# Block products in a feed-forward layer: sums of weight blocks on GpSimd, three pairs of k tiles instead of two

## Chip, cores and metric

One core of a Trainium2 chip runs the whole program: a two-layer encoder in float32, batch 1, 256 tokens, model width 2048. The metric is the device time of one execution in microseconds (us), the median of the runs shown.

## What is computed

The reference, cut to what the change touches. Before these lines each layer has three token mixers side by side (chunkwise mLSTM, latent attention, dilated attention) that share one input projection `w_in` and one output projection `w_out`.

```python
def hybrid_layer(x, ...):
    h = rms_norm(x, norm_mix)
    z = jnp.einsum('bsd,de->bse', h, w_in)
    ...                                   # the three mixers give y
    x = x + jnp.einsum('bse,ed->bsd', y, w_out)
    h = rms_norm(x, norm_ff)
    u = jax.nn.relu(jnp.einsum('bsd,df->bsf', h, w_ff1))
    return x + jnp.einsum('bsf,fd->bsd', u * u, w_ff2)
```

`w_ff1` is 2048 x 8192 and `w_ff2` 8192 x 2048, in each of two layers.

## The kernel before

**Products.** Every float32 operand is split into a high part that TensorE (PE) takes at full rate (`F32R`) and a remainder; a product is the three matmuls high x high, high x remainder, remainder x high. For the weights, `Weights.split` does this: ScalarE (ACT) casts a loaded unit `wst` (128 x 1024) to `whi`, VectorE (DVE) subtracts to get `wlo`. There are three buffers `wst` (`B_ST`) and four of `whi` and `wlo` each (`B_HL`), so the split of a unit can start once PE has used the unit four places before it. SyncE's queue (SP) issues the loads in the order of `weight_order`.

**Feed-forward.** `ffn` runs over four chunks of 2048 hidden columns. In a chunk, FF1 makes 16 tiles of 128 hidden columns, f0 to f15, each from two half units of `w_ff1` (`w_half`); `ff1_end` squares the ReLU, scales it and splits it into `u`. FF2 then makes four column groups of 512 output columns. The chunk is "quick" (`fast`) in three chunks of layer 0 and four of layer 1, and there two column groups are made at a time by `fast_groups`: g (left) and g+1 (right), each with two banks of PSUM, one for each half of the tokens.

**Block products.** For a pair `kp` of k tiles the product of a 2 x 2 block matrix of activations (two token halves by two k tiles) and a 2 x 2 block matrix of weights (two k tiles by two column groups) takes eight block products. For the pairs in `FAST = (2, 5)` it is made with seven, of sums of blocks: `act_sums` makes four sums of activation blocks on DVE, and `split` makes four sums of weight blocks, t1 to t4, on DVE from the blocks `a` (unit of the left group, "first") and `b` (unit of the right group, "second"). These make two more units to split, "sums" (t1, t2) and "more sums" (t3, t4). Four of the seven products gather in four banks `fast`, over both pairs, and at the end `fast_end` adds them to `x`, eight additions on DVE and one copy on ACT. The other six pairs are made plainly by `token_group`.

**Order.** The instructions of each engine stand in the order in which the program issues them. A planner (`Stream`) sets it at build time: it holds tasks with due times, worked out from a table of costs, and after each matmul it issues the tasks that are due. In `fast_groups` before, the left group runs through all pairs in order with both block pairs in their places, and then the right group runs through its six plain pairs.

Of the kernel before, what the change touches and what calls it, by code (L numbers as in the profile page):

```python
# [69 lines left out]
MARGIN = 0.3  # L70
ML_AT_ONCE = 2
WARM = 10
# [149 lines left out]
class Weights:  # L222
# [3 lines left out]
    def __init__(self, c, items):  # L226
        self.c, self.items = c, items
        self.srcs = [(i, src, n) for i, (src, n, kind) in enumerate(items) if src is not None]
        self.st, self.hl = {}, {}
        self.i = self.d = self.k = 0  # L230

    def load(self):
        c = self.c
        if self.d == len(self.srcs):
            return
        i, src, n = self.srcs[self.d]
        self.st[i] = c.wp.tile([P, 1024], F32, tag="wst", name="wst", bufs=c.B_ST)
        for cols in self.pieces(i):
            c.nc.sync.dma_start(self.st[i][:, cols], src[:, cols])
        self.d += 1  # L240

# [5 lines left out]
    def split(self):  # L247

        c, nc, k = self.c, self.c.nc, self.k
        src, n, kind = self.items[k]  # L250
        hi = c.wp.tile([P, 1024], F32R, tag="whi", name="whi", bufs=c.B_HL)
        lo = c.wp.tile([P, 1024], F32R, tag="wlo", name="wlo", bufs=c.B_HL)
        if kind == "sums":
            a, b = self.st.pop(k - 2), self.st.pop(k - 1)

            x, y = (c.big.tile([P, 1040], F32, tag="big", name="ws") for _ in range(2))
            self.st[k + 1] = y
            pieces, st = [slice(0, 512), slice(512, 1024)], x
        else:
            st = self.st[k] if kind else self.st.pop(k)  # L260
            if kind == "second":
                st = st[:, 512:]
                pieces = [slice(0, 512)]
            elif kind == "more sums":
                st = self.st.pop(k)
                pieces = [slice(0, 512), slice(512, 1024)]
            else:
                pieces = self.pieces(k)

        def parts():  # L270
            if kind == "sums":
# [5 lines left out]
            for cols in pieces:  # L277
                nc.scalar.copy(hi[:, cols], st[:, cols])
            yield
            for cols in pieces:  # L280
                nc.vector.tensor_tensor(out=lo[:, cols], in0=st[:, cols], in1=hi[:, cols].bitcast(F32),
                                        op=ALU.subtract)

        t = c.s.spawn(parts())
        if kind != "more sums":
            c.s.step(t)
        else:
            t.due = max(t.due, self.sums.due)
        if kind == "sums":
            self.sums = t  # L290
        self.hl[k] = (hi, lo, t)
        self.k += 1

    def next(self):
        while self.k < min(len(self.items), self.i + self.c.B_HL - 1):
            loads = self.items[self.k][0] is not None
            self.split()
            if loads:
                self.load()
        hi, lo, t = self.hl.pop(self.i)  # L300
        self.c.s.finish(t)
        self.i += 1
        return hi, lo
# [3 lines left out]
FAST = (2, 5)  # L307


def fast(l, ch, depth):  # L310
    return l == depth - 1 or ch < NCHUNK - 1


def weight_order(c, depth):
    srcs = []
    for l in range(depth):
# [8 lines left out]
        for ch in range(NCHUNK):  # L325
# [4 lines left out]
            for g in range(0, NX, 2):  # L330
                for kp in range(KT // 2):
                    if kp in FAST:
                        srcs += [(c.w_ff2[l, ch, g, kp], 1024, "first"), (c.w_ff2[l, ch, g + 1, kp], 1024, "second"),
                                 (None, 1024, "sums"), (None, 1024, "more sums")]
                    else:
                        srcs.append((c.w_ff2[l, ch, g, kp], 1024))
                srcs += [(c.w_ff2[l, ch, g + 1, kp], 1024) for kp in range(KT // 2) if kp not in FAST]
# [235 lines left out]
def layer_tables(c):  # L573
# [3 lines left out]
    rope = c.cp.tile([P, 4, NT, MLA_ROPE], F32, tag="rope", name="rope", bufs=1)  # L577
    drope = c.cp.tile([P, 2, NT, 4, DIL_ROT], F32, tag="drope", name="drope", bufs=1)
# [85 lines left out]
def k_rope(c, z1):  # L664
# [18 lines left out]
    kh = c.cp.tile([P, S], F32R, tag="krh", name="krh", bufs=1)  # L683
    kl = c.cp.tile([P, S], F32R, tag="krl", name="krl", bufs=1)
# [206 lines left out]
def ml_gates(c, z1):  # L891
# [60 lines left out]
    ahl = c.cp.tile([P, 2, S], F32R, tag="ml_ahl", name="ml_ahl", bufs=1)  # L952
# [171 lines left out]
def mixers(c, prepare, after):  # L1124
    nc, s = c.nc, c.s
    dv = c.cp.tile([P, 2, NT, DIL_H * DIL_DH], F32R, tag="dv", name="dv", bufs=1)
# [96 lines left out]
def ffn(c, l, last_layer, depth):  # L1223
# [3 lines left out]
    c.xss = new_ss(c)  # L1227
    for ch in range(NCHUNK):
# [3 lines left out]
        sums = {}  # L1232
        for f in range(KT):
# [5 lines left out]
            if i and kp in uf:  # L1239
                c.s.spawn(act_sums(c, us, kp, uf[kp], sums))  # L1240
        for g in range(0, NX, 2):
            last = last_layer and ch == NCHUNK - 1 and g == NX - 2
            if quick:
                fast_groups(c, us, sums, l, ch, g, last, last_layer, nxt)
# [8 lines left out]
def act_sums(c, us, kp, u, sums):  # L1253
# [5 lines left out]
    sf = tile2k(c, "sf", F32)  # L1259
# [5 lines left out]
    hl = c.big.tile([P, 1040], F32R, tag="big", name="s_hl")  # L1265
# [6 lines left out]
def fast_groups(c, us, sums, l, ch, g, last, last_layer, nxt):  # L1272
# [12 lines left out]
    banks = None  # L1285
    for kp in range(KT // 2):
        if kp not in FAST:
            token_group(c, us, left, 512, [kp])
            continue
        first, end = kp == FAST[0], kp == FAST[-1]  # L1290
        if first:
            right = two_banks(c)
            c.s.until(lambda: c.s.room["m"] >= 4)
            c.s.give(m=-4)
            banks = [new_bank(c, "fast") for _ in range(4)]
        p1, q5, p6, p7 = banks
        c.s.until(lambda: kp in sums)
        s1, s2, s3, s4 = sums[kp]
        w = c.w.next()
        product(p1, u(2 * kp, 0), w, one, first, end)  # L1300
        product(left[0], u(2 * kp + 1, 0), w, two, False, False)
        w = c.w.next()
        product(right[0], s4, w, one, first, False)
        w = c.w.next()
        product(q5, s1, w, one, first, end)
        product(p6, s2, w, two, first, end)
        w = c.w.next()
        product(p7, s3, w, one, first, end)
        product(left[1], u(2 * kp + 1, 1), w, two, False, False)
        if end:  # L1310
            done = c.s.spawn(fast_end(c, banks, g))
    c.s.spawn(ff2_end(c, left, g, l, ch, last_layer, nxt, done))
    kps = [kp for kp in range(KT // 2) if kp not in FAST]
    token_group(c, us, right, 512, kps[:-1] if last else kps, opened=(0,))
    if last:
        last_unit(c, us, right, 512)
    c.s.spawn(ff2_end(c, right, g + 1, l, ch, last_layer, nxt, done))

# [69 lines left out]
def encoder(ctx, tc, xT, x, const, vecs, w_in, w_in1, w_mla, w_out, w_ff1, w_ff2, out):  # L1388
# [31 lines left out]
    c.mean = c.cp.tile([P, 16], F32, tag="mean", name="mean")[:, :2]  # L1420
# [165 lines left out]
```

## Time and profile before

| | us |
|---|---|
| median of three runs (2107.16 to 2109.35) | 2108.2 |
| the profiled execution | 2108.59 |
| its span | 2106.8 |
| PE busy in it | 2094.5 |
| DVE busy | 1582.6 |
| ACT busy | 1125.8 |
| GpSimd (POOL) busy | 13.8 |
| DMA | 389.91 MB, mean 185 GB/s |

The profile is one execution; the quick chunks repeat each other, so that rows of one stand for all. Busy time is the time in which an engine had at least one instruction running; matmuls overlap, so that the duration of one (0.39 us for 512 columns) is longer than its distance from the next.

### The profile page before, as it was taken

The numbers are of one execution on the slowest core, as the hardware profiler recorded it, in microseconds if no ns is written. First come the engines' busy times: TensorE is split into PE (matmuls) and PEld (weight loads), VectorE is DVE, ScalarE is ACT, GpSimd is POOL, SyncE is SP. The second block draws the span as 40 slices with busy tenths as digits, with TensorE's granted clock in tenths as the row PEclk, the third lists the DMA queues.
The fourth block names the chain that finished last, engine by engine and source line by source line (L and its number), as shares of the span: only waits on it lengthen the run. The fifth ranks groups of instructions, "written<-read, shape, count | busy, mean of one in ns | idle before, by whom it ended". The sixth has DMA issues, their size and how long they took to land.

```text
span 2106.8 us, 29301 instructions
## 1 busy us (share of the span) xinstructions
PE 2094.5 (99%) x10792; PEld 1791.9 (85%) x10792; DVE 1582.6 (75%) x2624; ACT 1125.8 (53%) x1870; POOL 13.8 (1%) x35
## 2 busy tenths in 40 slices
PE   9999999999999999999999999999999999999999
PEld 8888888888888888888888888888888888888887
DVE  6789865788778778775557888567877787787786
ACT  5777654454455444544456675554544454454453
POOL 1000000000000000001000000000000000000000
PEclk9999999999999999999999999999999999999999
DMA  7544455666656665656555445556665566666665
GB/s 264 162 169 156 150 170 181 194 189 204 191 182 200 200 191 183 210 192 200 181 170 166 140 137 165 175 180 193 190 203 191 178 206 199 189 191 201 190 193 176
DMA packets 109151, 389.91 MB, mean 185 GB/s; under 512 B 12368, under 2 KB 12496, under 8 KB 108752
## 3 DMA queue, kind: packets, MB, share of 16 engines
q1 hardware_dynamic: 107136, 384.71, 57.8%
q10 hardware_dynamic: 1872, 3.33, 0.4%
q8 instruction: 84, 1.38, 0.3%
q14 instruction: 59, 0.48, 0.1%
HBM read 385.90 MB, written 2.10 MB: 184 GB/s over the span
## 4 chain that ended last, share of the span: by engine, by line
PE 95%; DMA 2%; DVE 1%; ACT 1%; issue 0%; ACTq 0%; DVEq 0%
PE g L200 85%; PE fast L200 4%; PE mla_z L200 2%; DMA wst<-w_in 1%; PE oT L200 1%; DVE wlo L104 1%; PE mla_s L200 1%; ACT whi L104 1%; PE ml_h L200 1%; PE pT L206 0%; PE xT L206 0%; PE dil_s L200 0%; DMA wst<-w_ff 0%; PE nkT L206 0%; PE dqkT L206 0%
## 5 line engine op out<-in xcount | busy, mean ns | idle before, releaser
L104 ACT CAST whi<-wst 128x1024 fp32r<-128x1024 f32 (+3 forms) x733 | 749.0, 1025 | 394.5 <-PE g L200 181.8
L104 DVE TENSOR_TENSOR wlo<-wst,whi 128x1024 fp32r<-128x1024 f32 (+3 forms) x733 | 863.6, 1189 | 127.4 <-ACT whi L104 125.5
L200 PE MATMUL g<-whi,u 128*128 128x512 f32 x1712 | 539.9, 390 | 0.0
L200 PE MATMUL g<-xg,whi 128*128 128x512 f32 x2048 | 489.9, 391 | 0.0
L200 PEld LDWEIGHTS g<-xg,whi 128*128 128x128 f32 x2048 | 376.7, 188 | 72.6
L200 PEld LDWEIGHTS g<-whi,u 128*128 128x128 f32 x1712 | 321.6, 188 | 66.7
L200 PE MATMUL g<-whi,xg 128*128 128x512 f32 (+1 forms) x1152 | 371.7, 389 | 1.8 <-ACT whi L104 1.8
L200 PE MATMUL g<-wlo,u 128*128 128x512 f32 x856 | 333.4, 389 | 0.0
L200 PEld LDWEIGHTS g<-xg,wlo 128*128 128x128 f32 x2048 | 262.9, 191 | 11.7 <-ACT xg L104 2.0
L200 PE MATMUL g<-xg,wlo 128*128 128x256 f32 x2048 | 267.4, 283 | 1.1 <-ACT xg L104 1.1
L200 PEld LDWEIGHTS g<-whi,xg 128*128 128x128 f32 x1152 | 215.2, 189 | 39.2 <-ACT whi L104 2.0
L200 PE MATMUL g<-wlo,xg 128*128 128x512 f32 (+1 forms) x576 | 221.0, 384 | 2.4 <-DVE wlo L104 2.4
L104 ACT COPY junk<-g 128x256 f32<-128x256 f32 x128 | 47.8, 373 | 304.9 <-PE g L200 304.9
L200 PEld LDWEIGHTS g<-wlo,u 128*128 128x128 f32 x856 | 160.9, 188 | 33.4
L104 DVE TENSOR_TENSOR junk<-g,junk 128x256 f32<-128x256 f32 x128 | 54.3, 424 | 173.8 <-ACT junk L104 173.8
L200 PE MATMUL g<-whi,y 128*128 128x512 f32 x512 | 164.7, 394 | 0.0
L200 PEld LDWEIGHTS g<-wlo,xg 128*128 128x128 f32 x576 | 109.2, 190 | 20.1 <-DVE wlo L104 3.8
L200 PEld LDWEIGHTS g<-whi,y 128*128 128x128 f32 x512 | 96.2, 188 | 19.4
L200 PE MATMUL g<-wlo,y 128*128 128x512 f32 x256 | 99.8, 390 | 0.0
L104 DVE TENSOR_TENSOR x<-g,x 128x512 f32<-128x512 f32 x80 | 53.4, 688 | 55.6 <-PE g L200 55.6
L104 ACT CAST whi<-ws 128x512 fp32r<-128x512 f32 x112 | 63.8, 619 | 40.5 <-PE g L200 40.5
L104 DVE TENSOR_TENSOR wlo<-ws,whi 128x512 fp32r<-128x512 f32 x112 | 71.7, 687 | 3.7 <-ACT whi L104 1.5
(244 smaller groups left out, 1693.1 us busy)
## 6 DMA issues: line engine op xcount, KB each, us to landing
wst<-w_ff SPq DMA_DIRECT2D x512, 512.0 KB, 4.2
wst<-w_in SPq DMA_DIRECT2D x127, 512.0 KB, 3.6
wst<-w_out SPq DMA_DIRECT2D x64, 512.0 KB, 4.0
wst<-w_in SPq DMA_DIRECT2D x16, 336.0 KB, 3.1
wst<-w_mla SPq DMA_DIRECT2D x12, 416.0 KB, 3.2
x<-x SPq DMA_DIRECT2D x2, 1024.0 KB, 6.0
out<-x ACTq DMA_DIRECT2D x8, 256.0 KB, 2.5
xt<-xT SPq DMA_DIRECT2D x7, 256.0 KB, 6.7
```

The costliest lines, as they stand in the source:

```text
L104: return fn(*args, **kw)
L200: c.nc.tensor.matmul(out, lhsT, rhs, start=start, stop=stop)
```

## The change

The third pair: `FAST` is (1, 3, 5). `fast_groups` no longer runs the left group to its end first, but follows the table `FAST_ORDER`: l is a plain unit of the left group, r one of the right group, b a block pair. The weight blocks of a pair are loaded into buffers of their own (pool `big`, four of them, that is two pairs; name `wab`), and `Weights.loads` lets up to three plain units and two pairs be on the way. The sums of weight blocks are issued when the pair's loads are, as four additions on GpSimd (`Weights.add`), t1 in place in `b`, the rest into a tile shared with the rope tables or other constants of the mixers and a tile of the pool `mla_zs`; the planner takes a landing time of 5 us (`LANDING`) and its cost of a GpSimd instruction to place the splits of the sums. The pairs of groups alternate in order from chunk to chunk (`pairs_order`), and where the last group of a chunk is the first of the next, the four banks `fast` stay open and are folded into `x` once for both (`goes_on`). The activation sums get a tile of their own. Ten warm-up matmuls at the program's start become fourteen.

```diff
+LANDING = 5.0
-WARM = 10
+WARM = 14
...
     def load(self):
...
+        if kind:
+            self.st[i] = c.big.tile([P, 1040], F32, tag="big", name="wab")
+        else:
+            self.st[i] = c.wp.tile([P, 1024], F32, tag="wst", name="wst", bufs=c.B_ST)
...
+        if kind == "second":
+            self.sum[i] = t = c.s.spawn(self.add(i))
+            t.last["dma"] = c.s.clk + LANDING
+            c.s.step(t)
+
+    def loads(self):
+
+        while self.d < len(self.srcs):
+            kind = self.srcs[self.d][3]
+            if kind != "second" and (self.out["pair"] == 2 if kind else self.out["plain"] == self.c.B_ST):
+                break
+            self.load()
+
+    def add(self, i):
+
+        c = self.c
+        a, b = self.st[i - 1], self.st[i]
+        self.mix = 1 - getattr(self, "mix", 1)
+        x = c.cp.tile([P, 1024], F32, tag=f"mix{self.mix}", name="ws", bufs=1)
+        y = c.zp.tile([P, 2 * WZ], F32, tag="mla_zs", name="ws")
+        t1, t2, t3, t4 = b[:, :512], x[:, :512], x[:, 512:], y[:, :512]
+        for out, p, q in ((t3, b[:, :512], b[:, 512:1024]), (t1, a[:, :512], b[:, :512]), (t2, t3, a[:, :512]),
+                          (t4, t2, a[:, 512:1024])):
+            c.nc.gpsimd.tensor_tensor(out=out, in0=p, in1=q, op=ALU.add)
+        self.st[i + 1], self.st[i + 2] = (t1, t2), (t3, t4)
...
-            if kind == "sums":
-                t1, t2, t3, t4 = x[:, :512], x[:, 512:1024], y[:, :512], y[:, 512:1024]
-                for out, p, q in ((t3, b[:, :512], b[:, 512:]), (t1, a[:, :512], b[:, :512]), (t2, t3, a[:, :512]),
-                                  (t4, t2, a[:, 512:])):
-                    nc.vector.tensor_tensor(out=out, in0=p, in1=q, op=ALU.add)
-                yield
...
+        if kind and "sums" in kind:
+            t.due = max(t.due, max(self.sum[k - 1 - (kind != "sums")].last.values()))
+        else:
             c.s.step(t)
...
-FAST = (2, 5)
+FAST = (1, 3, 5)
+FAST_ORDER = ('l0', 'b1', 'l2', 'r0', 'b3', 'l4', 'r2', 'b5', 'l6', 'l7', 'r4', 'r6', 'r7')
...
+def pairs_order(l, ch, depth):
+    return (2, 0) if ch % 2 and fast(l, ch, depth) else (0, 2)
+
+def goes_on(l, ch, g, depth):
+    return (ch + 1 < NCHUNK and fast(l, ch, depth) and fast(l, ch + 1, depth) and pairs_order(l, ch, depth)[1] == g
+            and pairs_order(l, ch + 1, depth)[0] == g)
...
+            first, end = kp == FAST[0], kp == FAST[-1] and not hold
+            if first:
+                right = two_banks(c)
+                if banks is None:
+                    c.s.until(lambda: c.s.room["m"] >= 4)
+                    c.s.give(m=-4)
+                    banks = [new_bank(c, "fast") for _ in range(4)]
+            new = first and held is None
```

On VectorE, at the end of FF1 in layer 0's first chunk and the start of its first FF2 group, this stands before (`junk_4717` is the last hidden tile, f15; `wlo<-wst` of 512 columns the second block of pair b2; `ws` the sums of weight blocks):

```order
L104 TENSOR_TENSOR junk_4717<-g,junk_4717 128x256
L104 SCALAR_TENSOR_TENSOR junk_4717<-junk_4717 128x256
L104 TENSOR_TENSOR junk_4717<-junk_4717,r_row 128x256
L104 TENSOR_TENSOR wlo<-wst,whi 128x512
L104 TENSOR_TENSOR ws<-wst 128x512 x2
L104 TENSOR_TENSOR ws<-ws,wst 128x512 x2
L104 TENSOR_TENSOR u<-junk_4717,u 128x256
L104 TENSOR_TENSOR wlo<-wst,whi 128x1024
L104 TENSOR_TENSOR wlo<-ws,whi 128x512 x4
```

and now, at the same place (`wlo<-wab` of 512 columns is the second block of pair b1 ahead of the last tile's chain, and its sum t1 behind it, `ws` its sums t2 to t4):

```order
L106 TENSOR_TENSOR wlo<-wab,whi 128x1024
L106 TENSOR_TENSOR u<-junk_4687,u 128x256
L106 TENSOR_TENSOR wlo<-wab,whi 128x512
L106 TENSOR_TENSOR junk_4741<-g,junk_4741 128x256
L106 SCALAR_TENSOR_TENSOR junk_4741<-junk_4741 128x256
L106 TENSOR_TENSOR junk_4741<-junk_4741,r_row 128x256
L106 TENSOR_TENSOR wlo<-wab,whi 128x512
L106 TENSOR_TENSOR wlo<-ws,whi 128x512 x3
L106 TENSOR_TENSOR u<-junk_4741,u 128x256
L106 TENSOR_TENSOR wlo<-wst,whi 128x1024 x2
```

The four additions of weight blocks have left VectorE, and the remainders of the sums follow the chain of the last tile directly.

On GpSimd this is new, directly after the mixers' last memset (one pair and the start of the next; 42 such pairs follow each other):

```order
L106 MEMSET ml_va 128x8
L106 TENSOR_TENSOR ws<-wab 128x512
L106 TENSOR_TENSOR wab<-wab 128x512
L106 TENSOR_TENSOR ws<-ws,wab 128x512 x2
L106 TENSOR_TENSOR ws<-wab 128x512
```

Each pair is t3, t1 (in place), t2 and t4; before, the memset was followed by nothing until the next layer's tables.

On SyncE's queue, where 256 loads `wst<-w_ff` of a layer followed each other, now the loads of pairs stand between those of plain units (33 are the 32 half units of FF1 and l0):

```order
L245 DMA wst<-w_ff 128x1024 x33
L245 DMA wab<-w_ff 128x1024 x2
L245 DMA wst<-w_ff 128x1024 x2
L245 DMA wab<-w_ff 128x1024 x2
L245 DMA wst<-w_ff 128x1024 x2
L245 DMA wab<-w_ff 128x1024 x2
L245 DMA wst<-w_ff 128x1024 x6
```

Pair b1 is issued right behind l0, b3 behind l2 and r0, b5 behind l4 and r2, and then l6, l7, r4, r6, r7 and the next group's l0.

## Rows read from the trace of the kernel before

**Rows 1.** The page's busy time, share of the span and instructions.

```profile
PE 2094.5 (99%) x10792; PEld 1791.9 (85%) x10792; DVE 1582.6 (75%) x2624; ACT 1125.8 (53%) x1870; POOL 13.8 (1%) x35
```

**Rows 2.** PE's waits, longest: total us, times, longest us.

```profile
PE g L200 <- DVE wlo L104: 2.4, 3, 1.3
PE g L200 <- ACT whi L104: 1.8, 1, 1.8
```

**Rows 3.** Timeline of PE, first FF2: start, duration (us), instruction, count.

```profile
447.29 0.39 PE L200 MATMUL g<-whi,u 128*128 128x512 f32 x1
...
452.73 0.39 PE L200 MATMUL fast<-whi,u 128*128 128x512 f32 x1
```

**Rows 4.** Program start: PE's timeline; stretches with busy us, granted clock (PEclk), DMA.

```profile
1.05 4.26 PE L559 MATMUL warm<-ones 128*128 128x128 f32 x20 [1.05 <-DVE mean L104]
7.12 0.50 PE L200 MATMUL g<-whi,xg 128*128 128x512 f32 x1 [1.80 <-ACT whi L104]
...
9.00:10.00 1.00, 1.00 (x4) 0.79 (x3) 0.69 (x2) 1.00 (x3) 0.00 (x0) 0.50 1.01 401
...
12.00:13.00 1.00, 1.00 (x6) 0.78 (x6) 1.00 (x2) 1.00 (x4) 0.00 (x0) 1.00 1.01 354
```

**Rows 5.** Stretches (FF2 group, FF1): length, busy PE, PEld, DVE, ACT, POOL, clock, DMA.

```profile
447.30:489.50 42.20, 42.20 (x187) 34.89 (x186) 34.69 (x46) 21.52 (x27) 0.00 (x0) 1.00 0.65 201
...
532.00:620.90 88.90, 88.90 (x513) 78.63 (x512) 65.89 (x105) 43.26 (x64) 0.00 (x0) 1.00 0.60 188
```

**Rows 6.** Groups of one shape, DVE and ACT: count, busy us, mean ns, idle before.

```profile
L104 DVE TENSOR_TENSOR wlo<-wst,whi 128x1024 fp32r<-128x1024 f32 x675 | 818.7, 1221 | 115.5 <-ACT whi L104 114.0
L104 DVE TENSOR_TENSOR wlo<-ws,whi 128x512 fp32r<-128x512 f32 x112 | 71.7, 687 | 3.7 <-ACT whi L104 1.5
...
L104 DVE TENSOR_TENSOR ws<-ws,wst 128x512 f32<-128x512 f32 x56 | 38.5, 688 | 1.0
L104 DVE TENSOR_TENSOR ws<-wst 128x512 f32<-128x512 f32 x56 | 36.0, 685 | 0.0
...
L104 DVE TENSOR_TENSOR wlo<-wst,whi 128x672 fp32r<-128x672 f32 x16 | 13.8, 872 | 10.4 <-ACT whi L104 10.3
...
L104 ACT CAST whi<-wst 128x1024 fp32r<-128x1024 f32 x675 | 708.0, 1051 | 364.8 <-PE g L200 165.8 <-DMA wst<-w_ff 130.0 <-DMA wst<-w_in 29.8
```

**Rows 7.** Timelines of POOL and DVE where the mixers' tables are made.

```profile
24.58 0.46 POOL L104 TENSOR_TENSOR rope<-const,vec 128x128 f32<-128x128 f32 x1
...
26.26 0.32 POOL L104 TENSOR_TENSOR drope<-const,vec 128x64 f32<-128x64 f32 x1
...
26.54 1.31 POOL L104 TENSOR_TENSOR drope<-const,vec 128x64 f32<-128x64 f32 x1
26.37 1.29 DVE L104 TENSOR_TENSOR wlo<-wst,whi 128x1024 fp32r<-128x1024 f32 x1 [2.47 <-ACT whi L104]
...
27.59 0.97 DVE L104 TENSOR_TENSOR wlo<-wst,whi 128x672 fp32r<-128x672 f32 x1
...
994.13 1.45 POOL L104 TENSOR_TENSOR rope<-const,vec 128x128 f32<-128x128 f32 x1
993.81 1.45 DVE L104 TENSOR_TENSOR wlo<-wst,whi 128x1024 fp32r<-128x1024 f32 x1 [0.85 <-ACT whi L104]
```

**Rows 8.** Timelines of ACT and DVE at the starts of two FF2 groups.

```profile
447.54 0.37 ACT L104 COPY junk<-g 128x256 f32<-128x256 f32 x1 [2.42 <-PE g L200]
...
448.87 0.43 DVE L104 TENSOR_TENSOR junk<-junk,r_row 128x256 f32<-128x256 f32 x1
449.21 0.69 DVE L104 TENSOR_TENSOR wlo<-wst,whi 128x512 fp32r<-128x512 f32 x1
...
489.10 1.37 DVE L104 TENSOR_TENSOR x<-g,x 128x512 f32<-128x512 f32 x2 [2.45 <-PE g L200]
```

**Rows 9.** DMA issues of the page: KB each, median us to landing.

```profile
wst<-w_ff SPq DMA_DIRECT2D x512, 512.0 KB, 4.2
```

More of the change, by code (lines that the diff above doesn't have):

```diff
@@ L227, in __init__ @@
         self.c, self.items = c, items
-        self.srcs = [(i, src, n) for i, (src, n, kind) in enumerate(items) if src is not None]
-        self.st, self.hl = {}, {}
+        self.srcs = [(i, *item) for i, item in enumerate(items) if item[0] is not None]
+        self.st, self.hl, self.sum = {}, {}, {}
+        self.out = dict(plain=0, pair=0)
         self.i = self.d = self.k = 0
@@ L233, in load @@
         c = self.c
[L234 to L237, printed above, removed]
+        i, src, n, kind = self.srcs[self.d]
+        if kind:
+            self.st[i] = c.big.tile([P, 1040], F32, tag="big", name="wab")
+        else:
+            self.st[i] = c.wp.tile([P, 1024], F32, tag="wst", name="wst", bufs=c.B_ST)
+        self.out["plain"] += not kind
+        self.out["pair"] += kind == "first"
         for cols in self.pieces(i):
@@ L284, in split @@
         t = c.s.spawn(parts())
-        if kind != "more sums":
+        if kind and "sums" in kind:
+            t.due = max(t.due, max(self.sum[k - 1 - (kind != "sums")].last.values()))
+        else:
             c.s.step(t)
[L287 to L290, printed above, removed]
+        self.out["plain"] -= not kind
+        self.out["pair"] -= kind == "more sums"
         self.hl[k] = (hi, lo, t)
@@ L1232, in ffn @@
         sums = {}
+        if quick:
+            hls = c.cp.tile([P, 2 * NT * DIL_H * DIL_DH], F32R, tag="dv", name="s_hl", bufs=1)
         for f in range(KT):
@@ L1284, in fast_groups @@
     left, right = two_banks(c), None
-    banks = None
-    for kp in range(KT // 2):
-        if kp not in FAST:
-            token_group(c, us, left, 512, [kp])
[L1289 to L1316, printed above, removed]
+    done, held = None, banks
+    for n, at in enumerate(FAST_ORDER):
+        kp = int(at[1])
+        more = [b[0] for b in FAST_ORDER[n + 1:]]
+        if at[0] == "b":
+            first, end = kp == FAST[0], kp == FAST[-1] and not hold
[6 more added lines that the diff above has]
+            new = first and held is None
+            p1, q5, p6, p7 = banks
+            c.s.until(lambda: kp in sums)
+            s1, s2, s3, s4 = sums[kp]
+            w = c.w.next()
+            product(p1, u(2 * kp, 0), w, one, new, end)
+            product(left[0], u(2 * kp + 1, 0), w, two, False, False)
+            w = c.w.next()
+            product(right[0], s4, w, one, first, False)
+            w = c.w.next()
+            product(q5, s1, w, one, new, end)
+            product(p6, s2, w, two, new, end)
+            w = c.w.next()
+            product(p7, s3, w, one, new, end)
+            product(left[1], u(2 * kp + 1, 1), w, two, False, False)
+            if end:
+                done = c.s.spawn(fast_end(c, banks, g))
+        elif at[0] == "l":
+            token_group(c, us, left, 512, [kp])
+            if "l" not in more:
+                c.s.spawn(ff2_end(c, left, g, l, ch, last_layer, nxt, done))
+        elif last and not more:
+            last_unit(c, us, right, 512)
+        else:
+            token_group(c, us, right, 512, [kp], opened=(0,))
```

79 lines of the change are left out of this document (37 added, 42 removed).

## Prediction

> **What bounds the kernel now.** Read the busy times first: TensorE (PE) is busy 99% of the span and VectorE (DVE) 75%, while GpSimd (POOL) is all but unused [rows 1]. Then the list of PE's waits: its longest entries add up to only a few microseconds in the whole run [rows 2]. So PE's stream of matmuls is the time. A removed matmul is worth its spacing, and each new wait of PE is paid in full. Third, the stretches: in the feed-forward layer the first product (FF1, from 532.0) holds DVE 66 of 89 us, and one group of the second product (FF2, from 447.3) holds it 34.7 of 42.2 us [rows 5]. DVE is the engine closest behind PE, and FF2 is where it is closest; there the change works.
>
> **Matmuls removed.** A pair of k tiles costs 8 x 3 matmuls of 512 columns, or 7 x 3 by the block products. A third pair in each of the 14 calls of `fast_groups` (three quick chunks in layer 0, four in layer 1, two calls each) takes away 14 x 3 = 42. From 447.29 to 452.73 are 24 matmuls [rows 3], so 0.227 us each: 42 x 0.227 = **-9.5 us**. No other term of the sum is this certain.
>
> **Warm-up.** 14 warm-up instructions in place of 10. The trace has 20 records for the 10, in 4.26 us; 28 take 6.0 us and end at 7.0, just ahead of the first real matmul at 7.12, so they delay nothing. [...] I take **-1.5**, bounds 0 and -1.6.
>
> **VectorE's own work.** It loses 112 weight additions (112 x 0.687 = 77 us) and, through the banks kept open, 5 of 14 folds with 8 additions each (about 27 us). It gains the remainders of the third pair: 70 more of 512 columns at 0.687 and 14 fewer of 1024 at 1.22, +31 us [rows 6]; and 7 more sets of activation sums, at most 5 x 0.69 each, +24. Net at least -49 us over 14 groups of 42 us, 3.5 us each. ScalarE gets 58 more instructions, but it is at 21.5 of 42.2 us in FF2 [rows 5] and its casts are as long in sum; nothing for that. The loads stay the same number of bytes; four buffers for pairs besides three for plain units can only make them earlier. Nothing for that either. If this were all, DVE would be relieved and the result would be 2108.6 - 9.5 - 1.5 = 2097.6.
>
> **What GpSimd's additions cost.** There are 42 x 4 = 168 additions of 512 columns. POOL's 128-column product lasts 0.46 us and a 64-column one 0.32 when DVE is quiet, 0.14 per 64 columns; 512 columns make an estimate of 0.46 + 6 x 0.14 = 1.30 us. That alone is 15.6 us in a group of 41.5. But look at the rows in which both engines work [rows 7]. A 64-column product of POOL that meets a remainder of DVE from 26.37 takes 1.31 in place of 0.32: it ends when DVE does. DVE's next remainder, 672 columns from 27.59, takes 0.97 against a mean of 0.872 for its form [rows 6], although POOL's share was a product of 0.28. At 993.81 DVE starts beside a 128-column product and takes 1.45 against 1.22, and POOL's next one takes 1.45 against 0.46. So the two do not share: they take turns, and DVE loses what is left of POOL's instruction less 0.1 to 0.2 us. By that reading a 512-column addition costs a DVE that is waiting about 1.30 - 0.2 = 1.1 us. The other reading is by share (0.10 of 0.28 up to 0.23 of about 0.4): 0.45 to 0.75 us each. The rows show no long POOL instruction, so both stay as bounds; I take 1.1, because every one of these rows fits the subtraction and only some fit a share.
>
> [...]
>
> All 168 at 1.1 are 185 us, more than the 49 that DVE gives back, but DVE has idle time and only what misses a deadline counts. So take the place with the least slack: the start of a group. Let 0 be the end of FF1 and the start of unit l0 (447.29). ScalarE starts its copy of the last FF1 tile at 447.54, and DVE is through with that tile's chain at 449.21, 1.92 us after [rows 8]. In the changed order the remainder of the first sum (t1) stands right behind, so it could end at 1.92 + 0.69 = 2.6. PE reads it after l0 (12 matmuls), the first block (6), the second (3) and one more: 22 x 0.227 = 4.99. The slack is 2.4 us. Into it fall POOL's four additions for the next pair, b3. Its loads stand behind that of r0, which takes the buffer of the last FF1 unit. That unit's split can start when a `whi` buffer is free, four half tiles of 88.9 / 32 = 2.78 us before 0 [rows 5], at -11.1, and is done a cast and a remainder (1.05 + 1.22 [rows 6]) later, at -8.8. A load lands 4.2 us after issue [rows 9], and two more of 512 KB behind it take 1.6 to 2.6 us each (320 or 200 GB/s): b3 is there at -1 to +1. Its four additions then alternate with DVE's remainders and steal up to 4 x 1.1 = 4.4 of 2.4 us. If three fall ahead of t1, PE waits 0.9 us; if all four, 2.0; where POOL is still at pair b1 and DVE already late, some 3.1. At the second group of a chunk DVE waits until the group before has ended (x<-g at 489.10 [rows 8]), two additions of 0.69 take the place of the chain, and the slack is the same 2.4; but these read PSUM and POOL can work beside them, so 0 to 2.2. Pair b5 lands during b3, behind l2 and r0 with more room, 0 to 1.2 us; I take 0. For a group start I take the middle of three and four additions, 1.4 us: 14 x 1.4 = **+19.6 us**, bounds 0 and 14 x 3.1 = 43.
>
> **Queues.** ScalarE's cast of t1 waits for POOL, and behind it stand the casts of t2 to t4, the last u and l2. The loads of pair b1 wait for a buffer that comes free two half tiles (5.6 us) earlier than that of b3, so b1 lands at about -6.5, and t1 and t2 are there after three additions with their turns (1.3 + 1.1 each), at +0.7; ScalarE is busy with the last tile's copy until then anyway. SP's loads of pairs wait for buffers that were free two pairs earlier. The banks kept open occupy all four of their kind during the next FF1, in which nobody asks for one. These cost nothing, and where they do it is the same wait of PE for a split.
>
> **The sum.** The profiled execution took 2108.6 us (span 2106.8 and 1.8 around it), 0.4 above the median of 2108.2. 2108.6 - 9.5 - 1.5 + 19.6 = 2117.2; I say **2117**.
>
> **Rivals.** (a) The cover holds: POOL works in DVE's 7 idle us a group and in the 3.5 freed, no deadline is missed. For it: DVE's load without POOL falls to about 31 of 41.5 us. Against it: 12 x 1.1 = 13 us then go into 10.5, and at a group's start into 2.4. 2097.6, with a few late splits up to 2101. (b) Turns cost by share, or b3 lands two additions earlier: 8 us of stalls, 2105.6, up to 2108; this is the case within 0.2%. (c) POOL's b1 additions run into those of b3 at every start: 3.1 us each, 2108.6 - 11 + 43 = 2141. [...] (d) The change does not do what it says: in the order of PE's instructions the 42 matmuls are gone, so no. The other side decides between (a) and the forecast at the point where a group start loses 11 / 14 = 0.8 us, which is three of the four additions ahead of t1.
>
> **How the numbers follow.** A measurement here tells about 0.2% from no change, 4.2 us: faster is below 2104, slower above 2112.4. Forecast with (c): stalls over 15 us, 0.48. (b): 0.19. (a): 0.33. The range leaves out a tenth at either side: low is (a) without any stall, 2097, high is near (c), 2138. By sign alone: where only slower cases count, 2113 to 2141.
>
> **What would show it.** [...] Wrong if PE's waits stay at a few us: then turns are cheaper, or POOL is done before 0. If the waits are for the sums by ScalarE on POOL, the loads were the fault and not the turns.

## The result, and the profile after

The changed kernel takes 2159.84 us (median of 4 runs, 2157.22 to 2163.01) beside 2107.85 of the kernel before: a ratio of 1.0249, interval 1.0236 to 1.0261. It is slower, the sign that the prediction held likeliest (0.48), but by 52 us and not by 9, and so outside the range of 2097 to 2138.

Page of the changed kernel, busy time, share of the span and instructions, to lay beside [rows 1]; and the longest of PE's waits (total us, times, longest us), beside [rows 2]:

```profile
PE 2107.3 (98%) x10758; PEld 1784.8 (83%) x10758; DVE 1658.3 (77%) x2563; ACT 1152.2 (53%) x1928; POOL 298.2 (14%) x203
```

```profile
PE fast L202 <- DVE wlo L106: 21.3, 19, 2.1
PE g L202 <- DVE wlo L106: 20.7, 25, 1.7
PE g L202 <- ACT whi L106: 2.2, 2, 1.5
```

PE has 34 instructions fewer: 42 matmuls gone, 8 warm-up records more. It now waits 42 us for `wlo` where it waited 3.2 (2.4 in [rows 2] and 0.8 in the products of the banks `fast`), and hardly more for ScalarE (2.2 for 1.8). VectorE is the engine that is late. It lost 112 additions and five folds, and yet it is busy 76 us longer. The groups by form (count, busy us, mean ns, idle before) say why, beside [rows 6]:

```profile
L106 DVE TENSOR_TENSOR wlo<-wst,whi 128x1024 fp32r<-128x1024 f32 x619 | 780.2, 1274 | 103.9 <-ACT whi L106 102.8
L106 POOL TENSOR_TENSOR ws<-ws,wab 128x512 f32<-128x512 f32 x84 | 151.5, 1804 | 3.3
L106 DVE TENSOR_TENSOR wlo<-ws,whi 128x512 fp32r<-128x512 f32 x126 | 112.9, 936 | 23.5 <-ACT whi L106 23.5
...
L106 DVE TENSOR_TENSOR wlo<-wab,whi 128x1024 fp32r<-128x1024 f32 x42 | 70.5, 1677 | 1.6 <-ACT whi L106 1.6
```

The same remainder of 512 columns takes 0.94 us on average in place of 0.69, that of 1024 columns of a pair 1.68 in place of 1.22, and an addition of t2 or t4 on POOL 1.80 where one that met nobody takes 1.31 (441.98 below).

**Where it happens.** The timelines of the first FF2 start, POOL, VectorE and PE of the changed kernel (start, duration, instruction). FF2's first matmul is at 448.45.

```profile
441.98 1.31 POOL L106 TENSOR_TENSOR ws<-wab 128x512 f32<-128x512 f32 x1 [409.07 <-DVE wlo L106]
443.37 1.30 POOL L106 TENSOR_TENSOR wab<-wab 128x512 f32<-128x512 f32 x1
444.63 2.92 POOL L106 TENSOR_TENSOR ws<-ws,wab 128x512 f32<-128x512 f32 x2
448.16 1.62 POOL L106 TENSOR_TENSOR ws<-wab 128x512 f32<-128x512 f32 x1 [0.62 <-DMA wab<-w_ff]
449.86 1.36 POOL L106 TENSOR_TENSOR wab<-wab 128x512 f32<-128x512 f32 x1
451.18 3.16 POOL L106 TENSOR_TENSOR ws<-ws,wab 128x512 f32<-128x512 f32 x2
```

```profile
444.00 0.95 DVE L106 SCALAR_TENSOR_TENSOR junk<-junk 128x256 f32<-128x256 f32 x1
444.99 1.40 DVE L106 TENSOR_TENSOR junk<-junk,r_row 128x256 f32<-128x256 f32 x1
446.31 2.31 DVE L106 TENSOR_TENSOR wlo<-wab,whi 128x1024 fp32r<-128x1024 f32 x1
448.55 1.51 DVE L106 TENSOR_TENSOR u<-junk,u 128x256 fp32r<-128x256 f32 x1
449.98 1.78 DVE L106 TENSOR_TENSOR wlo<-wab,whi 128x512 fp32r<-128x512 f32 x1
451.69 0.41 DVE L106 TENSOR_TENSOR junk<-g,junk 128x256 f32<-128x256 f32 x1
452.14 1.07 DVE L106 SCALAR_TENSOR_TENSOR junk<-junk 128x256 f32<-128x256 f32 x1
453.24 1.38 DVE L106 TENSOR_TENSOR junk<-junk,r_row 128x256 f32<-128x256 f32 x1
```

```profile
455.28 0.50 PE L202 MATMUL fast<-wlo,s_hl 128*128 128x512 f32 x1 [1.69 <-DVE wlo L106]
```

Eight additions run one behind the other, pair b1's four from 441.98 and pair b3's from 448.16. Every VectorE instruction with two inputs in SBUF that lies beside them loses half a us to 1.1, however short it is: 0.95 and 1.40 for 0.42, 1.51 for 0.42, 2.31 for 1.22, 1.78 for 0.68. The one that reads PSUM (`junk<-g`, 0.41) loses nothing. So the chain of the last FF1 tile begins at 451.69, 3.2 us after FF2's start, and PE stops inside the product of t1, for its remainder.

**How much.** From the first matmul of FF2 to the next FF1's first, a quick chunk took 84.4 to 84.8 us before and takes 90.55, 91.12, 92.59, 91.65, 95.9 and 93.23 now (the last chunk, with the program's end, 94.58 for 89.94). FF1 takes 89.07 in both. The seven stretches together are 52.2 us longer, of the 54.3 between the two profiled spans (2161.1 and 2106.8). Spacing of the matmuls less 0.227 us each, summed by place over the seven chunks: 22.1 us around b1 and l2 in the first group, 34.6 in the second group (4.1 at its first unit, the rest around b1 and l2), 7.9 at l4; elsewhere nothing. That is 64.6, the slower clock included; the kernel before had 3. Three of these places are starts of a group, as forecast; l4, behind b3, is not. In the first group PE stops at t1; in the second t1 is mostly there in time, and PE stops at t2, t3, t4 and l2. Ahead of the second start VectorE also has the fold of the first group, whose additions into `x` take turns with b1's (this line took 0.69 in e1):

```profile
488.43 1.45 DVE L106 TENSOR_TENSOR x<-x,junk 128x512 f32<-128x512 f32 x1
```

About 10 of these us are the clock. One drop in the changed kernel, as a stretch (length; busy PE, PEld, DVE, ACT, POOL; granted clock; DMA):

```profile
495.41:498.83 3.42, 3.42 (x10) 2.65 (x9) 3.42 (x5) 0.00 (x0) 2.39 (x2) 0.50 0.20 83
```

The granted clock is 0.50 there, where PE had just waited 1.92 us for `x` (to 494.57). Half of the 3.42 us is lost, 1.7. The profile has six such drops (at 495, 816, 1574, 1707, 1758 and 1891), none in FF1: 10.2 us. So 52.2 = -9.5 for the matmuls + 10.2 for the clock + 51.5 of stalls (64.6 - 10.2 - 3.0). This is the account of one execution, the slowest of the four, with a mean granted clock of 0.995; the two fastest (2157.22 and 2157.63) have 0.998 and 0.997, and lose less to drops. And the two terms are not independent: behind the drop at 495 us the second group loses 0.9 us at b1, in the other six chunks 2.3 to 4.2.

### The profile page after: what moved, and what is told of

It reads as the page before. It is cut to its first block, busy times and chain, and to the rows that moved or that the text cites. A ratio compares the mean times of both kernels' runs of the same rounds, so it can differ in the third digit from the quotient of the medians.

```text
span 2161.1 us, 29486 instructions
## 1 busy us (share of the span) xinstructions
PE 2107.3 (98%) x10758; PEld 1784.8 (83%) x10758; DVE 1658.3 (77%) x2563; ACT 1152.2 (53%) x1928; POOL 298.2 (14%) x203
## 4 chain that ended last, share of the span: by engine, by line
PE 77%; DVE 12%; issue 5%; DMA 3%; ACT 2%; ACTq 0%; DVEq 0%
PE g L202 69%; DVE wlo L106 8%; PE fast L202 2%; DVE junk L106 2%; DMA wst<-w_in 2%; ACT whi L106 2%; PE mla_z L202 2%; DMA wst<-w_ff 2%; DVE x L106 1%; PE oT L202 1%; PE mla_s L202 1%; PE ml_h L202 0%; DVE u L106 0%; PE pT L208 0%; PE xT L208 0%
## 5 line engine op out<-in xcount | busy, mean ns | idle before, releaser
L106 DVE TENSOR_TENSOR wlo<-wst,whi 128x1024 fp32r<-128x1024 f32 (+2 forms) x649 | 807.3, 1258 | 118.0 <-ACT whi L106 116.8
L106 ACT CAST whi<-wst 128x1024 fp32r<-128x1024 f32 (+2 forms) x649 | 668.1, 1038 | 247.9 <-DMA wst<-w_ff 88.0
L202 PE MATMUL g<-whi,u 128*128 128x512 f32 x1544 | 497.2, 393 | 1.9 <-DVE x L106 1.9
L202 PEld LDWEIGHTS g<-whi,u 128*128 128x128 f32 x1544 | 293.1, 190 | 63.7 <-ACT whi L106 2.3
L202 PE MATMUL g<-wlo,u 128*128 128x512 f32 x772 | 305.8, 396 | 16.8 <-DVE wlo L106 16.6
L106 POOL TENSOR_TENSOR ws<-wab 128x512 f32<-128x512 f32 x42 | 66.5, 1584 | 1674.0 <-DVE wlo L106 928.6
L106 ACT CAST whi<-wab 128x512 fp32r<-128x512 f32 (+1 forms) x126 | 96.2, 764 | 144.1 <-PE g L202 102.1
L106 DVE TENSOR_TENSOR junk<-g,junk 128x256 f32<-128x256 f32 x128 | 54.3, 424 | 151.2 <-ACT junk L106 151.2
L106 DVE TENSOR_TENSOR wlo<-wab,whi 128x512 fp32r<-128x512 f32 (+1 forms) x126 | 146.8, 1194 | 18.6 <-ACT whi L106 18.6
L106 POOL TENSOR_TENSOR ws<-ws,wab 128x512 f32<-128x512 f32 x84 | 151.5, 1804 | 3.3
L106 DVE TENSOR_TENSOR wlo<-ws,whi 128x512 fp32r<-128x512 f32 x126 | 112.9, 936 | 23.5 <-ACT whi L106 23.5
```

The costliest lines, as they stand in the source:

```text
L106: return fn(*args, **kw)
L202: c.nc.tensor.matmul(out, lhsT, rhs, start=start, stop=stop)
```

## The experiments

Every kernel was timed beside the kernel before on the same chip (2107.4, 2108.06, 2107.9 and 2108.01 us in the four sets). FF2 is the mean length of the six stretches above, the last left out; FF1 lies between 89.07 and 89.17 in all of them.

| kernel | us | ratio to before | FF2 |
|---|---|---|---|
| before | 2107.85 | 1 | 84.6 |
| after | 2159.84 | 1.0249 [1.0236, 1.0261] | 92.5 |
| e1_port_free | 2099.05 | 0.9965 [0.9949, 0.9980] | 83.0 |
| e2_dve_sums | 2124.49 | 1.0085 [1.0069, 1.0102] | 86.8 |
| e3_dose_on_before | 2144.99 | 1.0182 [1.0162, 1.0202] | 89.2 |
| e4_warm14 | 2107.40 | 1.0001 [0.9991, 1.0011] | 84.6 |
| e5_dve_sums_mended | 2120.03 | 1.0055 [1.0038, 1.0072] | 86.3 |
| e6_pair1_port_free | 2133.35 | 1.0124 [1.0109, 1.0139] | 87.9 |
| e7_pair3_port_free | 2116.40 | 1.0043 [1.0025, 1.0061] | 85.7 |
| e8_pieces128 | 2168.38 | 1.0286 [1.0271, 1.0302] | 93.0 |
| e9_dve_sums_spread | 2101.11 | 0.9969 [0.9957, 0.9980] | 83.5 |
| e10_pool_sums_spread | 2163.57 | 1.0263 [1.0250, 1.0277] | 92.2 |
| e11_dve_spread_no_hold | 2100.35 | 0.9967 [0.9956, 0.9979] | 83.7 |
| e12_two_pairs_pool | 2157.34 | 1.0232 [1.0214, 1.0250] | 91.4 |

**Is it the turns?** e1 leaves POOL's queue nearly as long as it was, but takes away most of what it reads (each sum is zeros but for 8 columns).

```diff
-            c.nc.gpsimd.tensor_tensor(out=out, in0=p, in1=q, op=ALU.add)
+            c.nc.gpsimd.tensor_tensor(out=out[:, :8], in0=p[:, :8], in1=q[:, :8], op=ALU.add)
+            c.nc.gpsimd.memset(out[:, 8:], 0.0)
+            c.nc.gpsimd.memset(out[:, 8:], 0.0)
```

> The changed kernel with each of the 168 GpSimd additions replaced by an 8-column addition and two memsets of 504 columns on GpSimd, which read nothing (the sums of weight blocks are left out, so the output is not the layer's). GpSimd is busy at the same places for about the same time, but hardly reads SBUF. Theory (GpSimd and VectorE take turns at a read port, the remainders come late): remainders of 1024 columns back at 1.22 us, every FF2 stretch 83 to 85 us instead of 90.6 to 95.9, about 2098 to 2103 us. Rival (the sums come late, or three pairs are simply too dense for VectorE): FF2 stretches stay above 90, about 2150 to 2160 us.

The same place in e1, POOL and VectorE:

```profile
447.72 1.10 POOL L106 MEMSET wab<- 128x504 f32 x2
```

```profile
447.16 0.42 DVE L106 TENSOR_TENSOR junk<-g,junk 128x256 f32<-128x256 f32 x1 [2.15 <-ACT junk L106]
447.62 0.44 DVE L106 SCALAR_TENSOR_TENSOR junk<-junk 128x256 f32<-128x256 f32 x1
```

POOL is busy 255.9 us here (298.2 in the changed kernel) at the same places, and VectorE's instructions have their old durations. The stalls are gone but for 1.5 us, and 2099.05 is what the sum gave for the matmuls alone (2097.6 to 2099.1, with and without the warm-up). Loads, casts, held banks and order thus cost next to nothing; the 60.8 us up to 2159.84 are the additions' reading. That the turns are taken at a port, as the theory has it, no row shows. That the sums come late is not it either: ScalarE waits for GpSimd's sums as little in the changed kernel (7.5 and 2.5 us in the whole run) as in e1 (7.0 and 2.2). The larger part of the first:

```profile
ACT whi L106 <- POOL ws L106: 7.5, 7, 1.7
```

VectorE's busy time is 1522.7 against 1658.3 us: 135.6 / 168 = 0.81 us for each addition on average, those that met an idle VectorE among them.

**The same additions where nobody uses them.** e3 is the kernel before with four additions on POOL that wait for the last `x<-g` of a pair of groups.

```diff
 def ff2_end(...):  # kernel before, at its end
+    if after and g % 2:
+        scratch = c.rope.rearrange("p a t d -> p (a t d)")
+        for i in range(4):
+            nc.gpsimd.tensor_tensor(out=scratch, in0=c.x[1][:, cols], in1=c.const[:, :512], op=ALU.add)
```

> The kernel before, with four GpSimd additions of 512 columns for which nobody waits, issued after each second column group pair's fold into x (56 in all: 28 at the start of the second FF2 group of the seven quick chunks, 28 at the start of FF1). Theory of turns: remainders near them take 2.0 to 2.5 us instead of 1.22, PE waits about 3 us at each second FF2 group, none in FF1: 7 x 3 = 21 us and some from a lower clock after the waits, 2125 to 2140 us. Rival (GpSimd's reads cost VectorE nothing, the additions only came late): 2107 to 2110 us.

It took 37.6 us more (2144.99 against 2107.4, two runs), above the 2125 to 2140 expected: each dose costs 3.8 us and not 3. One dose of four falls at the start of the second group and one at the start of FF1. POOL's dose in FF2 and what VectorE does beside it, the same three entries of the kernel before, and VectorE beside the dose in FF1 (POOL's four from 535.76):

```profile
489.71 7.24 POOL L104 TENSOR_TENSOR rope<-x,const 128x512 f32<-128x512 f32 x4 [458.58 <-DVE x L104]
```

```profile
489.49 2.91 DVE L104 TENSOR_TENSOR wlo<-wst,whi 128x1024 fp32r<-128x1024 f32 x2
492.33 3.47 DVE L104 TENSOR_TENSOR ws<-wst 128x512 f32<-128x512 f32 x2
495.72 2.49 DVE L104 TENSOR_TENSOR ws<-ws,wst 128x512 f32<-128x512 f32 x2
```

```profile
490.39 1.82 DVE L104 TENSOR_TENSOR wlo<-wst,whi 128x1024 fp32r<-128x1024 f32 x2
492.12 1.29 DVE L104 TENSOR_TENSOR ws<-wst 128x512 f32<-128x512 f32 x2
493.33 1.41 DVE L104 TENSOR_TENSOR ws<-ws,wst 128x512 f32<-128x512 f32 x2
```

```profile
535.53 5.69 DVE L104 TENSOR_TENSOR wlo<-wst,whi 128x1024 fp32r<-128x1024 f32 x3
```

In FF2 the three entries took 1.82, 1.29 and 1.41 us in the kernel before: 4.3 us lost to four additions. At FF1's start three remainders take 5.69 us for 3 x 1.22: 2.0 us in these alone. An FF2 stretch is 3.8 to 6.1 us longer than before (three of the six have a drop of the clock; the mean granted clock of the profiled execution is 0.996). FF1, where the splits run ahead, is as long as without, 89.07. So in both places a turn costs VectorE about 1 us, and it costs time only where VectorE has a deadline.

**Which turns?** e6 and e7 free one pair of the three, in the way of e1 (`self.pair` counts the pairs of a call; e6 has 0, which is b1, and e7 has 1, which is b3).

```diff
+            if self.pair in (0,):
+                ...  # 8 columns and two fills, as above
+                continue
             c.nc.gpsimd.tensor_tensor(out=out, in0=p, in1=q, op=ALU.add)
```

> The changed kernel, but the four additions of pair b1 alone are of 8 columns and followed by two fills of 504 columns on GpSimd (these rows of the sums are wrong, so part of the product is left out); b3 and b5 add as before. Theory A (turns of both pairs, eight in a row, use up one slack at the start of a group): with four turns fewer a start loses 4 us less, its stall is all but gone, 2100 to 2115. Theory B (only pair b3, as the prediction had it): the stall stays as it is, 2150 to 2160.

> The same for pair b3 alone; b1 and b5 add as before (part of the product is left out again). Theory A: as for b1, 2100 to 2115. Theory B (pair b3 alone is at fault): 2098 to 2103. Rival C (pair b1 alone, whose additions delay the last chain of FF1): 2145 to 2160.

Neither came out as any theory had it: 2133.35 and 2116.4. PE's idle places in the first chunk's first group, e6 and then e7:

```profile
453.98 0.50 PE L202 MATMUL fast<-wlo,s_hl 128*128 128x512 f32 x1 [0.62 <-DVE wlo L106]
```

```profile
466.21 0.50 PE L202 MATMUL g<-wlo,u 128*128 128x512 f32 x1 [1.12 <-DVE wlo L106]
```

VectorE in e6, up to the remainders of the first sums:

```profile
448.19 0.42 DVE L106 TENSOR_TENSOR junk<-g,junk 128x256 f32<-128x256 f32 x1 [2.15 <-ACT junk L106]
...
449.11 1.40 DVE L106 TENSOR_TENSOR junk<-junk,r_row 128x256 f32<-128x256 f32 x1
450.43 1.78 DVE L106 TENSOR_TENSOR wlo<-wab,whi 128x512 fp32r<-128x512 f32 x1
452.14 2.99 DVE L106 TENSOR_TENSOR wlo<-ws,whi 128x512 fp32r<-128x512 f32 x3
```

With b1's additions alone (e7) the start of the first group is free of waits in all seven chunks. With those of b3 (e6) it waits 0.9 us at b1 and 0.6 at l2 in the mean. With both it is 3.2. They add up against one slack, and the rows show how. In e6 the last chain begins 0.66 us after FF2 (447.53), as in e1, and meets three turns: 0.97 + 1.10 + 1.1 (2.99 for 1.89) = 3.2 us against the slack of 2.4. In this chunk two of them fall ahead of t1 (450.43), which PE still reads in time; the third falls on t2, read 0.68 us later with one more remainder to make, and there PE waits 0.62. In the changed kernel VectorE has by then lost 0.53 + 0.97 + 1.09 to b1's additions and 1.09 + 1.10 to the first two of b3: 4.8 us, of which the 2.15 us that it idles in e1 and e6 ahead of the chain take up a part. The chain begins 2.6 us late, loses 0.65 + 0.95 more, and 4.2 - 2.4 = 1.8 beside a wait of 1.69.

But e6 is still 34.3 us slower than e1, and most of that lies in the second group: 3.0 us a chunk at b1 and l2, with b1's turns gone. VectorE and PE at the first chunk's second start in e6 (the group begins at 491.28, b3's additions at 494.62):

```profile
494.93 5.19 DVE L106 TENSOR_TENSOR wlo<-ws,whi 128x512 fp32r<-128x512 f32 x3
500.04 3.44 DVE L106 TENSOR_TENSOR wlo<-wst,whi 128x1024 fp32r<-128x1024 f32 x2
```

```profile
498.49 0.50 PE L202 MATMUL fast<-wlo,s_hl 128*128 128x512 f32 x1 [0.70 <-DVE wlo L106]
500.17 0.50 PE L202 MATMUL g<-wlo,u 128*128 128x512 f32 x1 [0.72 <-DVE wlo L106]
502.40 0.50 PE L202 MATMUL g<-wlo,u 128*128 128x512 f32 x1 [1.27 <-DVE wlo L106]
```

Here all four turns fall behind t1, which PE reads in time, and the waits are for t3, t4 and l2. The first sum is not the only deadline: the remainders behind it have little more slack.

e7 has another thing: the waits at l4, 7.9 us in the changed kernel, are 13.9 there. They follow the additions of b5 (460.36 to 467.3 in e7), which had been taken for free; two remainders that take 2.37 us in e1 (462.07) take 4.54 beside them:

```profile
463.85 4.54 DVE L106 TENSOR_TENSOR wlo<-wst,whi 128x1024 fp32r<-128x1024 f32 x2
```

**Smaller pieces.** e8 cuts each addition into four.

```diff
-            c.nc.gpsimd.tensor_tensor(out=out, in0=p, in1=q, op=ALU.add)
+            for j in range(0, 512, 128):
+                s = slice(j, j + 128)
+                c.nc.gpsimd.tensor_tensor(out=out[:, s], in0=p[:, s], in1=q[:, s], op=ALU.add)
```

> The changed kernel with each addition of 512 columns cut into four of 128 on GpSimd. Theory of turns by instruction: a VectorE instruction loses at most 0.4 us instead of 1.1, but each of GpSimd's pieces has to wait for a VectorE instruction, so the sums of a pair take 15 us or more instead of 6 and come late: PE waits by way of the casts of the sums (whi), 2165 to 2250. Theory of a share of bandwidth: the same bytes, the same loss, 2155 to 2170, and waits for wlo as now.

VectorE in the last chain of FF1 in e8, and the longest of PE's waits in the whole run:

```profile
448.31 0.72 DVE L106 SCALAR_TENSOR_TENSOR junk<-junk 128x256 f32<-128x256 f32 x1
449.07 0.57 DVE L106 TENSOR_TENSOR junk<-junk,r_row 128x256 f32<-128x256 f32 x1
```

```profile
PE g L202 <- DVE wlo L106: 22.7, 60, 1.8
```

The time, 2168.38, lies in both expected ranges and decides nothing; the rows do. An instruction of VectorE now loses 0.1 to 0.3 us in place of 1, and the stall at b1 of the first group is gone. VectorE is busy 1587.2 us, 64.5 above e1 where the changed kernel is 135.6 above it. By a share of bandwidth, as the second theory has it, the same bytes would have cost the same. But POOL needs longer for a pair (0.69 to 0.90 us on average for a piece, 499.6 us busy in all), so the last sum, t4, comes late in b3 and b5 as well: ScalarE waits 151 us for GpSimd's sums here, 10 in the changed kernel. In sum it is slower than in one piece.

**Does a later reader help?** e10 puts a second plain unit ahead of b1 and one more between the pairs.

```diff
-FAST_ORDER = ('l0', 'b1', 'l2', 'r0', 'b3', 'l4', 'r2', 'b5', 'l6', 'l7', 'r4', 'r6', 'r7')
+FAST_ORDER = ('l0', 'l2', 'b1', 'r0', 'l4', 'b3', 'r2', 'l6', 'b5', 'l7', 'r4', 'r6', 'r7')
```

> The changed kernel with the same order of units and the additions still on GpSimd. Theory (turns against the slack at the start of a group): b1 is read 2.7 us later, but its loads and additions move back by a unit too; each pair's additions still fall into the splits of the pair ahead, so each stall becomes smaller by up to 2.7 us: 2110 to 2140. Rival (total turns are too many for VectorE wherever they fall, 168 x 1.05 us against about 10 us of idle in a group): 2140 to 2160.

It did not: 2163.57, above both ranges. The first group still stalls (2.16 us at the same product), and the second now waits before its first matmul, for a bank that VectorE has not emptied. PE's waits of e10:

```profile
PE g L202 <- DVE x L106: 16.5, 8, 3.6
```

b1's additions start 3.9 us ahead of FF2 (443.36) in place of 6.5, and still eight run in a row (to 456.7) through the chain. The remainder of the plain unit l2 has moved ahead of the chain too and takes turns there (2.33 us from 443.56).

**Two pairs only.** e12 undoes the third pair and its order, and keeps the rest.

```diff
-FAST = (1, 3, 5)
+FAST = (2, 5)
-FAST_ORDER = ('l0', 'b1', 'l2', 'r0', 'b3', 'l4', 'r2', 'b5', 'l6', 'l7', 'r4', 'r6', 'r7')
+FAST_ORDER = ('l0', 'l1', 'b2', 'l3', 'l4', 'b5', 'l6', 'l7', 'r0', 'r1', 'r3', 'r4', 'r6', 'r7')
```

> The changed kernel with two pairs in place of three: FAST = (2, 5) and the order of units of the kernel before, the additions still on GpSimd and the banks still held. So against the kernel before only the additions are moved (and folds saved); no matmul is gone. Theory (turns cost wherever their window holds a group's start): both pairs' loads may be out at once, so their eight additions run one after the other around the start of a group; the first sum is read after two plain units (5.4 us) in place of one, so each start stalls by 0.5 to 2 us less than the 3 to 4 of the changed kernel: 2107 + 14 x 1.5 to 3, 2128 to 2150. Rival (only the third pair's four turns are too many): 2104 to 2110.

2157.34, more than the 2128 to 2150 expected: 112 additions on GpSimd cost 49.3 us against the kernel before, 168 cost 60.8 against e1. In the first chunk eight run in a row around the start of either group (443.42 to 456.7, 491.03 to 504.5), since two pairs' loads may be out at once; VectorE at the second start of e12:

```profile
498.12 5.19 DVE L106 TENSOR_TENSOR wlo<-ws,whi 128x512 fp32r<-128x512 f32 x3
```

The three of 512 columns take 5.19 us in place of 1.89. The number of additions does not set the loss, but where they lie: e6, e7 and e12 have 112 of 512 columns each and lose 34.3, 17.4 (both against e1) and 49.3 us. That the eight in a row make e12 the dearest of the three is argued from these rows and not shown; holding back the second pair's loads until the first pair is read was not tried.

**The other parts.** e4 is the kernel before with `WARM = 14`.

```diff
-WARM = 10
+WARM = 14
```

> The kernel before with 14 warm-up instructions instead of 10. If the lower clock from 8 to 11.6 us cost 1.5 us that the longer warm-up gives back: FF2 of the first chunk starts at 445.8 instead of 447.3, 2106.5 us. If the first weights are what PE runs into at full clock, it starts at 447 to 448.5, and the time is 2107.5 to 2109.5 us.

```profile
9.00:10.00 1.00, 1.00 (x6) 0.79 (x5) 0.81 (x2) 1.00 (x3) 0.00 (x0) 1.00 1.02 393
```

Its stretch from 9 to 10 us has the clock at 1.00, against 0.50 in [rows 4], and PE's idle time ahead of 7.1 us is gone. But FF2 starts at 447.06, where it started at 447.29, and the time is the same to 0.1%, as the second case had it. The changed kernel has 1.50 us of that idle time and no drop either (1.00 from 9 to 13 us).

e2 and e5 bring the additions back to VectorE, into the split of the sums, and keep all else (the lines of the diff that add; `adds` are the four of a pair).

```diff
+            if kind == "sums":
+                for o, p, q in adds:
+                    nc.vector.tensor_tensor(out=o, in0=p, in1=q, op=ALU.add)
+                yield
```

> The changed kernel with the four additions of a pair moved back to VectorE, issued when the sums are split, as in the kernel before; three pairs, order and open banks stay. Theory of turns: VectorE's own load is 34 to 39 of 41.5 us a group but nothing stretches it; waits of 0 to 1.5 us a group, 2098 to 2118 us, no remainder above 1.3 us. Rival (three pairs are too dense): VectorE is still late at the start of each group, FF2 stretches above 90 us, above 2150 us.

In e2 the additions took the blocks of the pair loaded last instead of their own, so they also wait for a load that is not theirs; its 2124.49 us says little. e5 takes the right ones:

> The changed kernel with the twelve additions of a group on VectorE, each pair's four at the split of its sums, from the pair's own blocks; three pairs, the order of the units and the held banks stay. Theory (the time is lost to VectorE's waits for GpSimd's instructions): no PE wait of the kind seen now; VectorE's busy time in an FF2 group is about 39 of 41.5 us, so few stalls: 2098 to 2110. Rival (the three pairs themselves ask too much of VectorE in FF2, whoever adds): waits for wlo of about 1.5 us in each group, 2115 to 2127.

2120.03, the rival's time, though not for its reason. PE's waits of e5:

```profile
PE fast L202 <- DVE wlo L106: 18.4, 14, 1.9
```

Fourteen waits, one for each group, of 1.3 us on average: at the first start the pair's four additions, 0.69 us each (448.11 to 450.86), and a plain unit's remainder (1.22 from 451.11) stand ahead of the first sum, with one plain unit of matmuls as cover. So e9 is e5 with the spread order (the diff of e10), and e11 is e9 with `goes_on` returning False.

> The additions on VectorE, and in each group the order l0, l2, b1, r0, l4, b3, r2, l6, b5, l7, r4, r6, r7: one more plain unit ahead of each pair, 2.7 us of matmuls. Theory: what is left of the loss with the sums on VectorE is its four additions (2.75 us) at the start of a group, 1.5 to 2 us too late; with 2.7 us more of cover no PE wait is left: 2108 - 9.5 = 2096 to 2102. Rival: VectorE is full in FF2 and the stall only moves to a later pair: 2110 to 2122.

> As with the additions on VectorE and the spread order, but no banks are kept open from one chunk to the next: fourteen folds of the products in place of nine. Theory: the five folds more (eight additions and a copy each, 27 us of VectorE in all) fall where VectorE has about 2 us left in a group: 2 to 4 us each, 10 to 20 us over the run with held banks. Rival: they lie beside the tail of the group and the next FF1 and cost nothing: within 3 us of it.

Page of e9:

```profile
PE 2085.9 (99%) x10758; PEld 1781.2 (85%) x10758; DVE 1629.5 (78%) x2731; ACT 1148.1 (55%) x1928; POOL 14.0 (1%) x35
```

2101.11 us, 0.3% below the kernel before (0.9957 to 0.9980) and the fastest here that computes all of it, together with e11 (2100.35, the same within the intervals). The third pair gives 6.8 of the 9.5 us of its matmuls, and some 4 us of waits are left in FF2; VectorE had room for the additions after all. e10, with the same order and the additions on GpSimd, issued with the loads, takes 62 us more. The held banks are worth nothing: e11's five more folds lie beside other work.

## Why the prediction was right or wrong

- **Matmuls, -9.5: right.** e1 lies 8.4 below its kernel before (2107.4).
- **Warm-up, -1.5: wrong in size.** No run shows the 1.5 us: e4 measures 0, the bound that was given. The clock did come back (1.00 in place of 0.50 from 9 to 10 us), and was worth nothing at the end.
- **VectorE relieved by 49 us: right**, 60 in e1 (1582.6 to 1522.7).
- **An addition of 1.30 us, a turn of 1.1 us: right.** An addition alone takes 1.31; where VectorE meets one near its start, it loses 0.95 to 1.10. The estimate came from products of 128 and 64 columns [rows 7] and holds at 512. These rows and e8 (0.1 to 0.3 us beside pieces of 128 columns) show a turn by instruction, not a share, for VectorE's instructions with two inputs in SBUF.
- **"For a group start I take the middle of three and four additions, 1.4 us": this step failed.** It measured 51.5 / 14 = 3.7 us, l4's waits included. The landings were right: b1 was forecast at -6.5 and its additions start 6.5 us ahead of FF2, b3's at -1 to +1 and they start at -0.3. The step set b3's four additions alone against one deadline, t1, with a slack of 2.4 us at every start. Three things in it failed.
  - b1's additions were put under "Queues", where they "cost nothing". There only the readiness of the sums was asked, not whom POOL's reading delays. Their turns lie in the chains of the last FF1 tiles and use up VectorE's idle time before b3's begin, and two of b3's fall there too. Without them (e6) the time falls by 26.5 us. The text had this as rival (c), 3.1 us a start, at 2141 and so beyond its own range.
  - t1 is not the only deadline. For the first group the working was right: e6, with b3's turns alone, waits 1.5 us a start at b1 and l2. In its second group it waits 3.0, although PE reads t1 in time in six of the seven starts: t2, t3, t4 and l2 are late.
  - b5's turns were put at nothing (below).
- **The second group, "0 to 2.2": wrong.** 4.9 us with the clock (34.6 / 7). The slack is not "the same 2.4": the fold of the first group stands ahead on VectorE, and even in e1, without turns, t1 is ready only 1.4 us ahead of its reader in the first chunk. The fold's own additions into `x` (both inputs in SBUF) and the splits take turns too; only the PSUM readers are free, as was said of them: `junk<-g` takes 0.424 us in the mean before and after, `x<-g` 0.688 and 0.684, `junk<-fast` 0.684 and 0.683.
- **b5 "I take 0": wrong**, 7.9 us at l4, by the same kind of turns; 0.6 a start, inside the 0 to 1.2 that was allowed for it.
- **The clock: left out of the sum and of the range.** 10 us. [rows 4] has the granted clock at 0.50 behind a wait of 1.80 us; in the changed kernel such a drop costs 1.7 us, six times.
- **What would show it: neither sign against the forecast came.** PE's waits did not stay at a few us: 42 us for `wlo`, and PE's idle time rose by 41.5 us (2161.1 - 2107.3 against 12.3). ScalarE waits 10.0 us for POOL's sums in the whole run, so the loads were not at fault. POOL's additions of t2 and t4 take 1.80 us in the mean, and VectorE is not less busy but 76 us more.

Put together, for the profiled execution: -9.5 + 0 + 51.5 + 10.2 = +52.2, against -9.5 - 1.5 + 19.6 = +8.6. The sign came out as forecast and by the mechanism that was forecast, turns ahead of VectorE's deadlines; but the stalls were put at little more than a third of what they measured.

## What to carry to other kernels

Before work goes to an engine that takes turns with a busy one, count its instructions that fall into the window ahead of each deadline of the busy engine, all of them, also those whose results are early, and each deadline, not the first alone; multiply by what one of them costs the busy engine; only then subtract slack. Work taken off the busy engine that made it wait in turns was no relief here: four additions of 0.69 us on VectorE (e5, e9) were cheaper than four on GpSimd that cost it up to 1.1 us each. In this kernel VectorE itself was the cheap place for the sums once their reader stood one unit later (e9).

## What the hardware showed that was not expected

- A GpSimd fill (`MEMSET`, no input) cost VectorE nothing: 0.42 to 0.44 us beside fills of 1.10 for two (e1), against 0.95 to 1.51 beside additions. The fills write 504 columns each and the additions 512; what sets them apart here is the reading.
- The short instruction pays as much as the long one: 0.42 becomes 1.51 and 1.22 becomes 2.31 beside the same additions.
- Four of the six drops of the granted clock to 0.50 in the changed kernel came after single waits of 1.9 to 2.1 us, and two (1574 and 1758 us) beside three waits of 0.72 to 1.25 us with matmuls between them. But a wait of 2.10 us at 2073.80 in the same profile was followed by none (1.00 from 2070 to 2080 us), and e6, whose longest wait is 1.9 us, has a mean granted clock of 1.000 in its profiled execution. What decides it these runs don't show.
